# Last k tile of the first chunk tile by tile, evacuations ahead of low parts, a halved first cast, and more slots in a side list: one hybrid layer on one Trainium2 core

## The chip, the cores and the metric

The kernel runs on one core of one Trainium2 chip (trn2). The metric is the device time of one launch in microseconds (us); lower is better. All arithmetic is fp32. Products are made exact enough by splitting each fp32 operand into a high part (rounded to the format fp32r, one pass through TensorE) and a low part (the remainder), and by adding three products: high x high, high x low and low x high.

## The reference, cut to what matters

One layer over 1024 prompt tokens and 64 sample tokens (8 sequences of 8), model width 1024:

```
h    = rmsnorm(x, g_norm)                       # 1088 tokens x 1024
proj = h @ w_in                                 # 3200 columns = 25 tiles of 128
bg, cg, v, zA, a, g, zB, q, zX = split(proj)
out_A = bg * dwconv3(cg * v) * silu(zA)
out_B = silu(layernorm(dwconv31(a * sigmoid(g)))) * silu(zB)
out_X = softmax(q k^T / 8) v * silu(zX)         # 4 heads, 256 memory tokens
y     = rmsnorm(x + concat(out_A, out_B, out_X) @ w_out, g_final)
```

The prompt's keys and values come from `mem_prompt`; each of the eight sample sequences has its own cached keys and values. The states of both convolutions and the prompt's keys and values are outputs too.

## The kernel before, in words

**Tiles.** The projection is computed transposed: an accumulator in PSUM holds 128 output columns by a chunk of tokens, and eight k tiles of 128 input channels are summed in it. The first four column tiles ("head", `NHEAD`; three of kind `a`, one of kind `g`) go over four token chunks of 256, 256, 256 and 320 (`HEAD`); the other 21 over three of 384, 384 and 320 (`REST`). Per tile and chunk TensorE makes 24 matmuls: pass 0 is high weights x high tokens (rows `mm<-hh,wh`), pass 1 low weights x high tokens (`mm<-hh,wl`), pass 2 high weights x low tokens (`mm<-hl,wh`). `pass_k(n, c, acc, p, k)` is one of them. PSUM has eight banks: four for these accumulators (`MM`, rows named `mm`) and four for everything else (`SD`, rows named `sd`).

**Who does what.** TensorE (PE) also transposes the tokens (`x_tr`, rows `sd<-ident,x`). ScalarE (ACT) takes such a bank and writes the high part `hh` (`x_ev_hi`), VectorE (DVE) the low part `hl` (`x_ev_lo`). Weights are loaded in fp32 (`wr`); a CAST makes `wh` and VectorE the remainder `wl`. For the first four column tiles the weights come per k tile: `hw_hi(k)` casts 128x512, columns of all four tiles side by side, and `hw_lo(k)` subtracts. Only k tile 0 is cast by VectorE, the others by ScalarE (`S.copy`).

**The start.** `startup()` (L1007) is written out by hand, and each engine runs its part of it in the order of the code. Chunks 0 and 1 are multiplied without their norm factor; it is applied when an accumulator is emptied. For this `r_bc` makes diagonal matrices of the factors on VectorE, `r_tr` transposes them on TensorE, and a copy puts the row into `rrow`; `evac` of a head tile in chunks 0 and 1 is then one VectorE multiplication by `rrow` (rows `u<-mm,rrow` for the three tiles of kind `a`, `sig<-mm,rrow` for the `g` tile). `n0` and `n1` are the norms of chunks 0 and 1: `square(i)` is a ScalarE pass over one 128x1024 token tile (rows `junk<-x`), `chain` and `factor` are small VectorE operations. After chunk 0 has used its accumulators, chunk 1 gets the same four banks; its first matmul per tile thus waits for that tile's evacuation. Chunk 1 starts with pass 0 of all four tiles, k tile by k tile, with one pair of transposes (`x_tr(1, k + 4)`) behind each of the first four.

**The rest.** Outside `startup()` a list scheduler sets each engine's order from the code's order and readiness. Beside the main stream there is a queue of side steps: `side()` is called twice in each pass of eight matmuls (after k = 3 and k = 7) and runs the next entry; an entry `None` is an empty slot. The samples' attention is such a series, queued at column tile 14 (L1249): transposes of the cached keys (`sa_T`), `sa_scores`, `S0` empty slots, `sa_norm` (VectorE scales the softmax rows `Ps`), `S1` empty slots, `sa_pT` (TensorE transposes `Ps`, VectorE copies the result to `Pts`), `S2` empty slots, `sa_pv` (product with the cached values, ScalarE copies to `Os`), `S3` empty slots, `sa_out` (TensorE transposes `Os`). `st_out`, the output of the convolution states, is queued behind it. The 31 taps of the long convolution are VectorE operations on 128x1024 (rows `accB<-u,prm,accB`), a few per tile.

Of the kernel before, what the change touches and what calls it, by code (L numbers as in the profile page):

```python
# [23 lines left out]
SCALE = 0.125  # L24
NBIG = 45
A0, A1, A2, A3, A4, A5 = 2, 9, 5, 3, 3, 1
S0, S1, S2, S3 = 4, 3, 4, 2
L0, L1, L2 = 1, 3, 2
T1, T2, T3 = 2, 2, 3
TAPPRI = 100  # L30
# [11 lines left out]
def hybrid_trunk_kernel(  # L42
# [32 lines left out]
    def nm(s):  # L75
        uid[0] += 1
        return f"{s}_{uid[0]}"

    def B(s, dt=F32, cols=NT):
        return big.tile([128, cols], dt, tag="b", name=nm(s))  # L80

    def SD():
        return sdp.tile([128, 512], F32, tag="s", name=nm("sd"))

    def MM():
        return mmp.tile([128, 512], F32, tag="m", name=nm("mm"))
# [7 lines left out]
    def mm(out, lhsT, rhs, start, stop, cost):  # L94
        T.matmul(out, lhsT, rhs, start=start, stop=stop)  # L95
        pe_t[0] += cost
# [4 lines left out]
    def tr(out, in_, n):  # L101
        T.transpose(out, in_, ident[:n, :n])  # L102
        pe_t[0] += 107

    def dv(ns):
        dve_t[0] += ns
# [128 lines left out]
    def x_tr(c, k):  # L235
        off, n = HEAD[c]
        ps = SD()
        for i in groups[c]:
            o = xcols[i] - off
            tr(ps[:, o:o + 128], xt[i][:, k * 128:(k + 1) * 128], 128)  # L240
        return ps

    def x_ev(c, k, ps):
        x_ev_hi(c, k, ps)
        x_ev_lo(c, k, ps)

    def x_ev_hi(c, k, ps):
        off, n = HEAD[c]
        S.activation(hh[k][:, off:off + n], ps[:, :n], AF.Copy, scale=gT[:, k:k + 1])  # L249

    def x_ev_lo(c, k, ps):
        off, n = HEAD[c]
        V.scalar_tensor_tensor(
            hl[k][:, off:off + n], ps[:, :n], gT[:, k:k + 1],
            hh[k][:, off:off + n].bitcast(F32), ALU.mult, ALU.subtract,
        )
        dv(n / 0.96 + 130)
# [14 lines left out]
    hrw, hwh, hwl = [None] * 4, [None] * 4, [None] * 4  # L272

    def hsl(k):
        return slice((k % 2) * 512, (k % 2) * 512 + 512)
# [7 lines left out]
    def hw_hi(k, copy):  # L283
        if k % 2 == 0:
            hwh[k // 2] = B("wh", F32R, D)
            hwl[k // 2] = B("wl", F32R, D)
        copy(hwh[k // 2][:, hsl(k)], hrw[k // 2][:, hsl(k)])  # L287

    def hw_lo(k):
        V.tensor_sub(hwl[k // 2][:, hsl(k)], hrw[k // 2][:, hsl(k)], hwh[k // 2][:, hsl(k)].bitcast(F32))  # L290
# [2 lines left out]
    def w_block(n, k, lo):  # L293
        if n < NHEAD:
            o = (k % 2) * 512 + n * 128
            return (hwl if lo else hwh)[k // 2][:, o:o + 128]
        return (wlo if lo else whi)[n][:, k * 128:(k + 1) * 128]
# [95 lines left out]
    def chunks(n):  # L393
        return HEAD if n < NHEAD else REST
# [108 lines left out]
    def ev_z(c, ps, kk, src):  # L503
        off, n, p, s = pieces(c)
        if c[0] == 0:
            sz[0] = B("sz")
            mh[kk] = B("mh", F32R, SEQ)
            ml[kk] = B("ml", F32R, SEQ)
        m = src[:, off:off + n]
        S.activation(sz[0][:, off:off + n], ps[:, :n], AF.Silu)  # L510
        V.tensor_tensor(m, sz[0][:, off:off + n], m, ALU.mult)
        S.copy(mh[kk][:, off:off + p], m[:, :p])
        V.tensor_sub(ml[kk][:, off:off + p], m[:, :p], mh[kk][:, off:off + p].bitcast(F32))
        dv(2 * n / 0.96 + 140)
        if s:
            hi = ms[0][:, kk * 128:kk * 128 + 64]
            lo = ms[0][:, kk * 128 + 64:kk * 128 + 128]
            S.copy(hi, m[:, p:n])
            V.tensor_sub(lo, m[:, p:n], hi.bitcast(F32))
            dv(140)  # L520

    def evac(n, c, ps):
        kind, j, _ = order[n]
        c = chunks(n)[c]
        rawc[0] = n < NHEAD and c[0] < RAW
        if kind == "zA":
            ev_z(c, ps, j, tA[j])
        elif kind == "zB":
            ev_z(c, ps, 3 + j, accB[j])
        elif kind == "zX":  # L530
            ev_z(c, ps, 6 + j, aO[j])
        else:
            {"g": ev_g, "a": ev_a, "q": ev_q, "cg": ev_cg, "v": ev_v, "bg": ev_bg}[kind](c, ps, j)

    def pass_k(n, c, ps, p, k, last=2):
        off, N = chunks(n)[c]
        h = hl if p == 2 else hh
        mm(
            ps[:, :N], w_block(n, k, p == 1), h[k][:, off:off + N],
            p == 0 and k == 0, p == last and k == KT - 1, N / 2.4,  # L540
        )
# [465 lines left out]
    def startup():  # L1007
# [25 lines left out]
        n0, n1, n2, n3 = (Norm([xt[i] for i in g], [xrows[i] for i in g]) for g in groups)  # L1033
# [3 lines left out]
        def r_bc(norm, off):  # L1037
            norm.chain()
            norm.factor()
            for i in (0, 1):  # L1040
                o = off + i * 128
                V.tensor_scalar(rrow[0][:, o:o + 128], ident, 0.0, norm.f[:, i:i + 1], ALU.mult, ALU.add)
            dv(500)
# [20 lines left out]
        def p(k, j):  # L1064
            for n in range(NHEAD):
                pass_k(n, 0, acc[n], j, k, 1)
# [7 lines left out]
        def late(k):  # L1074
            banks.append(SD())
            for i in (0, 1):
                x0_tr(k, i)

        hw_hi(0, V.tensor_copy)
        hi(0)  # L1080
        hi(1)
# [3 lines left out]
        for i in (0, 1):  # L1085
            x0_tr(3, i)
        hw_hi(1, S.copy)
        lo(1)
        hw_lo(1)
# [4 lines left out]
        lo(2)  # L1094
        p(1, 0)
        hw_hi(2, S.copy)
        hw_lo(2)
        lo(3)
# [44 lines left out]
        t1 = [x_tr(1, 0), x_tr(1, 1)]  # L1143
# [4 lines left out]
        p(6, 1)  # L1148
        rps = r_tr(0)
        S.copy(rrow[0][:, RAW:RAW + 256], rps[:, :256])  # L1150
        n1.square(0)
        t1 += [x_tr(1, 2), x_tr(1, 3)]
        p(7, 0)
        x_ev(1, 2, t1[2])
        x_ev(1, 3, t1[3])
        n1.square(1)
        for n in range(NHEAD):
            for j in (2, 1):
                pass_k(n, 0, acc[n], j, KT - 1, 1)
            evac(n, 0, acc[n])  # L1160
        acc = [MM() for _ in range(NHEAD)]
        for k in range(KT):
            if k > 3:
                x_ev(1, k, t1[k])
            for n in range(NHEAD):
                pass_k(n, 1, acc[n], 0, k)
            if k + 4 < KT:
                t1.append(x_tr(1, k + 4))
            if k == 3:
                r_bc(n1, 256)  # L1170
        n2.square(0)
        n2.square(1)
        n2.chain()
# [23 lines left out]
    if True:  # L1197
        with tc.manual_schedule():
            startup()
# [16 lines left out]
        for n in range(NHEAD, NCT):  # L1216
            w_load(n + 2)
            kind, j, _ = order[n]
# [137 lines left out]
```

## Time and profile before

| what | value |
|---|---|
| median of 3 runs (lowest to highest) | 473.11 us (472.13 to 474.51) |
| the profiled execution | 472.01 us |
| its span, first to last instruction | 470.2 us |
| mean granted TensorE clock | 0.996 |
| busy: PE / weight loads (PEld) / DVE / ACT | 459.7 / 435.1 / 333.4 / 229.5 us |
| chain that ended last, by engine | PE 86%, DVE 11%, DMA 1%, issue 1%, ACT 1% |

The profiled execution lies 1.1 us under the median, and 1.8 us of it lie outside the span. PEld is the loading of the stationary operand, which overlaps the matmuls. Times in the rows are us from the span's start; a row of the timeline gives start, duration, engine, line of the code, operation, output<-inputs, shapes and count, and in brackets how long the engine sat idle before it and what ended that. All VectorE instructions are issued through one wrapper and stand at L59, nearly all matmuls at L95, transposes at L102.

### The profile page before, as it was taken

The numbers are of one execution on the slowest core, as the hardware profiler recorded it, in microseconds if no ns is written. First come the engines' busy times: TensorE is split into PE (matmuls) and PEld (weight loads), VectorE is DVE, ScalarE is ACT, GpSimd is POOL, SyncE is SP. The second block draws the span as 40 slices with busy tenths as digits, with TensorE's granted clock in tenths as the row PEclk, the third lists the DMA queues.
The fourth block names the chain that finished last, engine by engine and source line by source line (L and its number), as shares of the span: only waits on it lengthen the run. The fifth ranks groups of instructions, "written<-read, shape, count | busy, mean of one in ns | idle before, by whom it ended". The sixth has DMA issues, their size and how long they took to land.

```text
span 470.2 us, 7495 instructions
## 1 busy us (share of the span) xinstructions
PE 459.7 (98%) x2931; PEld 435.1 (93%) x2931; DVE 333.4 (71%) x593; ACT 229.5 (49%) x584; POOL 4.2 (1%) x20
## 2 busy tenths in 40 slices
PE   8999999999999999999999989999999999999994
PEld 8899999999999999999999879999999888888884
DVE  4769999999878999996899965237353537333333
ACT  5785659600223648565795364595542534111112
POOL 2000000000000000000000000000000000000000
PEclk9999999999999999999999999999999999999998
DMA  8931253100460300422021102113401634311111
GB/s 295 370 93 46 71 153 91 45 1 0 128 187 16 119 1 1 135 57 80 12 79 46 43 3 62 45 46 105 164 2 45 233 147 129 118 45 46 45 67 68
DMA packets 36447, 40.44 MB, mean 86 GB/s; under 512 B 1743, under 2 KB 30453, under 8 KB 36405
## 3 DMA queue, kind: packets, MB, share of 16 engines
q1 hardware_dynamic: 35965, 39.21, 25.7%
q10 hardware_dynamic: 448, 0.76, 0.5%
q8 instruction: 23, 0.38, 0.3%
q14 instruction: 11, 0.09, 0.1%
HBM read 34.81 MB, written 5.42 MB: 86 GB/s over the span
## 4 chain that ended last, share of the span: by engine, by line
PE 86%; DVE 11%; DMA 1%; issue 1%; ACT 1%; ACTq 0%; DVEq 0%
PE mm L95 76%; DVE accB L59 6%; PE sd L95 5%; PE sd L102 4%; DVE tA L59 1%; DVE wl L59 1%; DMA wr<-in_w_in_dram 1%; DVE red L59 1%; PE sd L874 1%; DVE mx L59 0%; DVE s L59 0%; ACT junk L187 0%; DVE hl L59 0%; ACT yg L997 0%; ACTq L1011 0%
## 5 line engine op out<-in xcount | busy, mean ns | idle before, releaser
L95 PE MATMUL mm<-hh,wh 128*128 128x384 f32 (+2 forms) x632 | 118.9, 324 | 1.1 <-DVE u L59 0.8
L95 PE MATMUL mm<-hl,wh 128*128 128x384 f32 (+2 forms) x632 | 118.6, 323 | 0.0
L59 DVE SCALAR_TENSOR_TENSOR accB<-u,prm,accB 128x1024 f32<-128x1024 f32 x90 | 115.4, 1282 | 1.5
L95 PE MATMUL mm<-hh,wl 128*128 128x384 f32 (+2 forms) x632 | 116.4, 321 | 0.0
L95 PEld LDWEIGHTS mm<-hh,wh 128*128 128x128 f32 x632 | 101.9, 188 | 2.8 <-DVE u L59 1.0
L95 PEld LDWEIGHTS mm<-hl,wh 128*128 128x128 f32 x632 | 101.7, 188 | 0.7 <-issue 0.6
L95 PEld LDWEIGHTS mm<-hh,wl 128*128 128x128 f32 x632 | 101.6, 188 | 0.4
L95 PE MATMUL mm<-woh,ml 128*128 128x512 f32 (+1 forms) x136 | 51.2, 377 | 0.0
L95 PE MATMUL mm<-wol,mh 128*128 128x512 f32 (+1 forms) x136 | 51.2, 377 | 0.0
L95 PE MATMUL mm<-woh,mh 128*128 128x512 f32 (+1 forms) x136 | 51.2, 377 | 0.0
L59 DVE TENSOR_TENSOR xres<-mm,xres 128x512 f32<-128x512 f32 (+2 forms) x19 | 12.4, 662 | 39.7 <-PE mm L95 39.5
L952 ACT ACTIVATE sd<-xres 128x512 f32<-128x512 f32 (+1 forms) x16 | 9.6, 600 | 57.9 <-DVE xres L59 57.9
L59 DVE TENSOR_TENSOR wl<-wr,wh 128x512 fp32r<-128x512 f32 x50 | 33.4, 688 | 4.2 <-ACT wh L287 2.2
L95 PEld LDWEIGHTS mm<-woh,mh 128*128 128x128 f32 x136 | 25.6, 188 | 4.7
L95 PEld LDWEIGHTS mm<-woh,ml 128*128 128x128 f32 x136 | 25.6, 188 | 4.7
L95 PEld LDWEIGHTS mm<-wol,mh 128*128 128x128 f32 x136 | 25.6, 188 | 4.6
L310 ACT CAST wh<-wr 128x512 fp32r<-128x512 f32 x42 | 24.4, 620 | 1.7 <-issue 1.3
L362 ACT ACTIVATE prod<-us,prm 128x64 f32<-128x64 f32 x93 | 24.9, 345 | 0.1
L510 ACT ACTIVATE sz<-mm 128x384 f32<-128x384 f32 (+1 forms) x24 | 11.4, 474 | 23.3 <-PE mm L95 23.1
L712 ACT ACTIVATE P<-sd,nb 128x256 f32<-128x256 f32 x32 | 14.7, 473 | 13.2 <-DVE nb L59 12.3
L433 ACT ACTIVATE sig<-mm 128x384 f32<-128x384 f32 (+1 forms) x6 | 2.8, 474 | 37.4 <-PE mm L95 37.3
L249 ACT ACTIVATE hh<-sd,gT 128x256 fp32r<-128x256 f32 (+1 forms) x32 | 14.3, 491 | 7.1 <-PE sd L102 6.8
(198 smaller groups left out, 527.9 us busy)
## 6 DMA issues: line engine op xcount, KB each, us to landing
wr<-in_w_in_dram SPq DMA_DIRECT2D x21, 512.0 KB
wor<-in_w_out_dram SPq DMA_DIRECT2D x8, 512.0 KB
xres<-in_x_prompt_dram SPq DMA_DIRECT2D x8, 512.0 KB
out_dram<-xres SPq DMA_DIRECT2D x7, 512.0 KB
x<-in_x_prompt_dram SPq DMA_DIRECT2D x6, 512.0 KB
cache<-in_cache_mem_k_dram SPq DMA_DIRECT2D x8, 256.0 KB
cache<-in_cache_mem_v_dram SPq DMA_DIRECT2D x8, 256.0 KB
wr<-in_w_in_dram SPq DMA_DIRECT2D x6, 256.0 KB
```

Source lines behind the costliest of these rows:

```text
L59: r = f(*a, **k)
L95: T.matmul(out, lhsT, rhs, start=start, stop=stop)
L102: T.transpose(out, in_, ident[:n, :n])
L249: S.activation(hh[k][:, off:off + n], ps[:, :n], AF.Copy, scale=gT[:, k:k + 1])
L310: S.copy(dst_hi[:, a:b], src[:, a:b])
L362: S.activation(p3[:, k, :], src, AF.Copy, scale=w[:, k0 + k:k0 + k + 1])
L433: S.activation(sig[j][:, off:off + n], ps[:, :n], AF.Sigmoid)
L510: S.activation(sz[0][:, off:off + n], ps[:, :n], AF.Silu)
L712: S.activation(P_[i][:, h * 256:h * 256 + 256], bank[h // 2][:, (h % 2) * 256:(h % 2) * 256 + 256], AF.Exp, bias=nb[:, h:h + 1], scale=SCA ...
L874: T.transpose(ps[:, j * 128:j * 128 + 128], accB[j][:, lncols[i]:lncols[i] + 128], ident)
L952: S.activation(junk[:rows], xr[:rows, cs], AF.Square, accum_out=ss[:rows, f:f + 1])
```

## The change

Three edits. (1) `hw_hi(0)`, the first weight cast, is made as two casts of 128x256. (2) In `startup()` the last k tile of chunk 0 (k = 7) is no longer pass 0 of all four tiles followed by passes 2 and 1 tile by tile, but all three passes tile by tile. The transposes of chunk 1's k tiles 2 and 3 stand ahead of it and behind its first tile. The low parts of those two (`x_ev_lo`) stand behind the four evacuations, the two squares of `n1` move back (the second to behind k = 4 of chunk 1), and `r_bc(n1, 256)` moves behind chunk 1's pass 0. (3) `S1` goes from 3 to 7 and `S2` from 4 to 6.

```diff
--- before.py
+++ after.py
@@ -24,7 +24,7 @@
 SCALE = 0.125
 NBIG = 45
 A0, A1, A2, A3, A4, A5 = 2, 9, 5, 3, 3, 1
-S0, S1, S2, S3 = 4, 3, 4, 2
+S0, S1, S2, S3 = 4, 7, 6, 2
 L0, L1, L2 = 1, 3, 2
 T1, T2, T3 = 2, 2, 3
 TAPPRI = 100
@@ -284,7 +284,11 @@
         if k % 2 == 0:
             hwh[k // 2] = B("wh", F32R, D)
             hwl[k // 2] = B("wl", F32R, D)
-        copy(hwh[k // 2][:, hsl(k)], hrw[k // 2][:, hsl(k)])
+        c0 = (k % 2) * 512
+        for a in (range(c0, c0 + 512, 256) if k == 0 else ()):
+            copy(hwh[0][:, a:a + 256], hrw[0][:, a:a + 256])
+        if k:
+            copy(hwh[k // 2][:, hsl(k)], hrw[k // 2][:, hsl(k)])
 
     def hw_lo(k):
         V.tensor_sub(hwl[k // 2][:, hsl(k)], hrw[k // 2][:, hsl(k)], hwh[k // 2][:, hsl(k)].bitcast(F32))
@@ -1148,16 +1152,18 @@
         p(6, 1)
         rps = r_tr(0)
         S.copy(rrow[0][:, RAW:RAW + 256], rps[:, :256])
-        n1.square(0)
-        t1 += [x_tr(1, 2), x_tr(1, 3)]
-        p(7, 0)
-        x_ev(1, 2, t1[2])
-        x_ev(1, 3, t1[3])
-        n1.square(1)
+        t1.append(x_tr(1, 2))
+        x_ev_hi(1, 2, t1[2])
         for n in range(NHEAD):
-            for j in (2, 1):
+            for j in (0, 2, 1):
                 pass_k(n, 0, acc[n], j, KT - 1, 1)
+            if n == 0:
+                t1.append(x_tr(1, 3))
+                x_ev_hi(1, 3, t1[3])
+                n1.square(0)
             evac(n, 0, acc[n])
+        x_ev_lo(1, 2, t1[2])
+        x_ev_lo(1, 3, t1[3])
         acc = [MM() for _ in range(NHEAD)]
         for k in range(KT):
             if k > 3:
@@ -1166,8 +1172,9 @@
                 pass_k(n, 1, acc[n], 0, k)
             if k + 4 < KT:
                 t1.append(x_tr(1, k + 4))
-            if k == 3:
-                r_bc(n1, 256)
+            if k == 4:
+                n1.square(1)
+        r_bc(n1, 256)
         n2.square(0)
         n2.square(1)
         n2.chain()
```

TensorE at the last k tile of chunk 0. The accumulators are mm_40 to mm_43; `hh_27`, `hl_28` are k tile 7's tokens, `sd_75`/`sd_76` before and `sd_74`/`sd_75` now the transposes of chunk 1's k tiles 2 and 3. Before:

```order
L102 MATMUL sd_76_374<-ident_72,x_6_109 128x128
L102 MATMUL sd_76_374<-ident_72,x_8_114 128x128
L95 MATMUL mm_40_168<-hh_27_138,wh_62_309 128x256
L95 MATMUL mm_41_169<-hh_27_138,wh_62_309 128x256
L95 MATMUL mm_42_170<-hh_27_138,wh_62_309 128x256
L95 MATMUL mm_43_171<-hh_27_138,wh_62_309 128x256
L95 MATMUL mm_40_168<-hl_28_139,wh_62_309 128x256
L95 MATMUL mm_40_168<-hh_27_138,wl_63_310 128x256
L95 MATMUL mm_41_169<-hl_28_139,wh_62_309 128x256
L95 MATMUL mm_41_169<-hh_27_138,wl_63_310 128x256
L95 MATMUL mm_42_170<-hl_28_139,wh_62_309 128x256
L95 MATMUL mm_42_170<-hh_27_138,wl_63_310 128x256
```

Now:

```order
L102 MATMUL sd_74_370<-ident_72,x_6_109 128x128
L102 MATMUL sd_74_370<-ident_72,x_8_114 128x128
L95 MATMUL mm_40_168<-hh_27_138,wh_62_310 128x256
L95 MATMUL mm_40_168<-hl_28_139,wh_62_310 128x256
L95 MATMUL mm_40_168<-hh_27_138,wl_63_311 128x256
L102 MATMUL sd_75_377<-ident_72,x_6_109 128x128
L102 MATMUL sd_75_377<-ident_72,x_8_114 128x128
L95 MATMUL mm_41_169<-hh_27_138,wh_62_310 128x256
L95 MATMUL mm_41_169<-hl_28_139,wh_62_310 128x256
L95 MATMUL mm_41_169<-hh_27_138,wl_63_311 128x256
L95 MATMUL mm_42_170<-hh_27_138,wh_62_310 128x256
L95 MATMUL mm_42_170<-hl_28_139,wh_62_310 128x256
```

The second pair of transposes moved behind the first tile's three matmuls, and each accumulator is complete three matmuls after the one before it.

VectorE at the same place; `u` and `sig` are the evacuations, `hl_18` and `hl_20` the low parts of chunk 1's k tiles 2 and 3. Before:

```order
L59 TENSOR_TENSOR wl_63_310<-wr_7_111,wh_62_309 128x512
L59 SCALAR_TENSOR_TENSOR hl_14_125<-sd_71_343,gT_74,hh_13_124 128x256
L59 SCALAR_TENSOR_TENSOR hl_16_127<-sd_72_346,gT_74,hh_15_126 128x256
L59 SCALAR_TENSOR_TENSOR hl_18_129<-sd_75_371,gT_74,hh_17_128 128x256
L59 SCALAR_TENSOR_TENSOR hl_20_131<-sd_76_374,gT_74,hh_19_130 128x256
L59 TENSOR_TENSOR u_78_389<-mm_40_168,rrow_35_155 128x256
L59 TENSOR_TENSOR u_79_394<-mm_41_169,rrow_35_155 128x256
L59 TENSOR_TENSOR u_80_399<-mm_42_170,rrow_35_155 128x256
L59 TENSOR_TENSOR sig_81_404<-mm_43_171,rrow_35_155 128x256
```

Now:

```order
L59 TENSOR_TENSOR wl_63_311<-wr_7_111,wh_62_310 128x512
L59 SCALAR_TENSOR_TENSOR hl_14_125<-sd_71_344,gT_74,hh_13_124 128x256
L59 SCALAR_TENSOR_TENSOR hl_16_127<-sd_72_347,gT_74,hh_15_126 128x256
L59 TENSOR_TENSOR u_77_383<-mm_40_168,rrow_35_155 128x256
L59 TENSOR_TENSOR u_78_389<-mm_41_169,rrow_35_155 128x256
L59 TENSOR_TENSOR u_79_395<-mm_42_170,rrow_35_155 128x256
L59 TENSOR_TENSOR sig_80_401<-mm_43_171,rrow_35_155 128x256
L59 SCALAR_TENSOR_TENSOR hl_18_129<-sd_74_370,gT_74,hh_17_128 128x256
L59 SCALAR_TENSOR_TENSOR hl_20_131<-sd_75_377,gT_74,hh_19_130 128x256
```

Two low parts stood ahead of the four evacuations and now stand behind them.

TensorE at the samples' softmax, column tiles 17 (its last chunk, 128x320) and 18 (128x384). Before, the two pairs of transposes of `Ps` stand within pass 2 of tile 17's last chunk:

```order
L95 MATMUL mm_3120<-hl_129,wh_2860 128x320
L95 MATMUL mm_3120<-hl_131,wh_2860 128x320
L102 MATMUL sd_3144<-ident,Ps_3079 128x128 x2
L95 MATMUL mm_3120<-hl_133,wh_2860 128x320
L95 MATMUL mm_3120<-hl_135,wh_2860 128x320
L95 MATMUL mm_3120<-hl_137,wh_2860 128x320
L95 MATMUL mm_3120<-hl_139,wh_2860 128x320
L102 MATMUL sd_3153<-ident,Ps_3086 128x128 x2
```

Now they stand within pass 1 of tile 18's first chunk:

```order
L95 MATMUL mm_3157<-hh_128,wl_3052 128x384
L95 MATMUL mm_3157<-hh_130,wl_3052 128x384
L102 MATMUL sd_3170<-ident,Ps_3080 128x128 x2
L95 MATMUL mm_3157<-hh_132,wl_3052 128x384
L95 MATMUL mm_3157<-hh_134,wl_3052 128x384
L95 MATMUL mm_3157<-hh_136,wl_3052 128x384
L95 MATMUL mm_3157<-hh_138,wl_3052 128x384
L102 MATMUL sd_3179<-ident,Ps_3087 128x128 x2
```

Between the two places lie 16 matmuls: the last four of 128x320 and twelve of 128x384. `sa_pv`, `sa_out` and `st_out` move by six slots (24 matmuls). Behind this place ScalarE's order has the copies `Os` behind the two casts of tile 19's weights, where they stood ahead of them. From column tile 19 on the order of every engine is as before.

## The prediction

> **What bounds the kernel now.** I read the page first (busy time, chain), then PE's waits, then busy time by stretch, and last the timeline at each wait.
>
> ```profile
> PE 459.7 (98%) x2931; PEld 435.1 (93%) x2931; DVE 333.4 (71%) x593; ACT 229.5 (49%) x584; POOL 4.2 (1%) x20
> PE 86%; DVE 11%; DMA 1%; issue 1%; ACT 1%; ACTq 0%; DVEq 0%
> ```
>
> PE is busy for 459.7 of 470.2 us. None of the edits removes a matmul, so all that can be won is PE's idle time, 10.5 us, or time that passes for busy.
>
> ```profile
> PE sd L102 <- DVE Ps L59: 1.3, 1, 1.3
> PE mm L95 <- DVE u L59: 0.8, 1, 0.8
> PE mm L95 <- DVE wh L59: 0.3, 1, 0.3
> PE sd L102 <- ACT rrow L1150: 0.2, 1, 0.2
> ```
>
> Columns: who waited for whom, us in total, times, longest. They are the places of the three edits: the first cast (`wh`), the copy of `rrow` and the evacuations (`u`) at the end of chunk 0, and the samples' softmax (`Ps`).
>
> ```profile
> core 0: us, PE busy (x) PEld busy (x) DVE busy (x) ACT busy (x) POOL busy (x), PEclk, DMA share, GB/s
> 18.30:36.80 18.50, 17.41 (x140) 16.32 (x139) 13.87 (x40) 15.07 (x31) 0.00 (x0) 1.00 0.48 150
> 36.80:58.40 21.60, 21.60 (x173) 21.37 (x174) 20.95 (x44) 11.80 (x28) 0.00 (x0) 1.00 0.20 58
> 58.40:225.00 166.60, 166.60 (x1075) 163.77 (x1076) 153.45 (x217) 81.52 (x230) 0.20 (x2) 1.00 0.24 72
> 225.00:260.00 35.00, 35.00 (x271) 34.07 (x270) 34.50 (x43) 25.17 (x75) 0.10 (x1) 1.00 0.16 46
> 260.00:275.00 15.00, 14.23 (x110) 12.68 (x108) 14.79 (x21) 8.47 (x14) 0.00 (x0) 1.00 0.13 36
> 287.00:464.00 177.00, 176.86 (x958) 160.66 (x956) 77.97 (x182) 69.13 (x170) 0.00 (x0) 1.00 0.25 85
> ```
>
> From 36.8 to 260 us PE has no idle time, and from 287 to 464 us only 0.14. What is won at the start reaches the end if DVE, as full as PE from 225 on (34.50 of 35.00 us), follows.
>
> **Edit 1, the first cast in halves.**
>
> ```profile
> 5.78 0.84 ACT L249 ACTIVATE hh<-sd,gT 128x256 fp32r<-128x256 f32 x2 [2.05 <-PE sd L102]
> 5.94 0.43 DVE L59 CAST wh<-wr 128x512 fp32r<-128x512 f32 x1 [0.37 <-DMA wr<-in_w_in_dram]
> 6.28 0.48 DVE L59 SCALAR_TENSOR_TENSOR hl<-sd,gT,hh 128x256 fp32r<-128x256 f32 x1
> 6.51 0.72 PE L95 MATMUL mm<-hh,wh 128*128 128x256 f32 x4 [0.34 <-DVE wh L59]
> 7.29 0.62 ACT L287 CAST wh<-wr 128x512 fp32r<-128x512 f32 x1 [0.67 <-DMA wr<-in_w_in_dram]
> 8.12 0.55 PEld L95 LDWEIGHTS mm<-hh,wh 128*128 128x128 f32 x4
> ```
>
> The cast ends at 6.37 and the first matmul starts 0.14 later. No row shows a cast of 256; it lies between half of 0.43 and 0.43 whole, about 0.29. The first half then ends at 6.23, so PE starts by up to 0.14 earlier (`hh` is ready at about 6.2). But the next weights are cast on ACT, which waited for their DMA and ends at 7.91; with the same 0.1 of signalling their LDWEIGHTS cannot come before 8.02, where it now comes at 8.12. So 0.10 is left of it. What waits behind the second half on DVE is `hl`: it starts before its predecessor has ended (6.28 against 6.37), so it slips by some 0.07, and PE needs it only later. Ends: 0.15 if the second half delays what follows by its whole length, turned into a loss (+0.15), and 0.34, the whole idle time. I take -0.10, the bound that the next cast's row sets.
>
> [...]
>
> **Edit 2, the last k tile of chunk 0.**
>
> ```profile
> 18.12 0.69 DVE L59 TENSOR_TENSOR wl<-wr,wh 128x512 fp32r<-128x512 f32 x1
> 18.43 0.38 PE L102 MATMUL sd<-ident,x 128*128 128x128 f32 x2
> 18.62 0.37 ACT L1150 COPY rrow<-sd 128x256 f32<-128x256 f32 x1 [1.07 <-PE sd L102]
> 18.72 0.87 DVE L59 SCALAR_TENSOR_TENSOR hl<-sd,gT,hh 128x256 fp32r<-128x256 f32 x2
> 18.89 1.06 ACT L187 ACTIVATE junk<-x 128x1024 f32<-128x1024 f32 x1
> 19.05 0.44 PE L102 MATMUL sd<-ident,x 128*128 128x128 f32 x2 [0.24 <-ACT rrow L1150]
> 20.45 0.88 DVE L59 SCALAR_TENSOR_TENSOR hl<-sd,gT,hh 128x256 fp32r<-128x256 f32 x2 [0.85 <-ACT hh L249]
> 21.24 1.08 DVE L59 TENSOR_TENSOR u<-mm,rrow 128x256 f32<-128x256 f32 x3
> 21.71 1.38 PE L95 MATMUL mm<-hh,wh 128*128 128x256 f32 x4 [0.80 <-DVE u L59]
> 22.23 0.42 DVE L59 TENSOR_TENSOR sig<-mm,rrow 128x256 f32<-128x256 f32 x1
> 22.93 0.38 PE L102 MATMUL sd<-ident,x 128*128 128x128 f32 x2
> 23.06 0.71 PE L95 MATMUL mm<-hh,wh 128*128 128x256 f32 x4
> ```
>
> The chain: a square on ACT (18.89) holds up the high parts, those hold up two low parts on DVE (idle 0.85, then 20.45), those the evacuations (21.24 on), and PE waits 0.80 for the first. Its next four matmuls take 1.38 against 0.71 for four at 23.06: they too come one evacuation apart, 0.33, which the idle column doesn't show.
>
> Now the same rows in the new order, in the old times. Transposes at 18.43, three matmuls at 18.65, 18.77 and 18.89 (0.12 apart: 256 columns against the 384 that take 1.48 for eight at 276.54 below), the third just behind `wl` (18.12 + 0.69 = 18.81). The second pair of transposes waits for the copy of `rrow` as before and stays at 19.05. The nine matmuls behind it run from 19.24 and complete the second, third and fourth accumulator at about 19.85, 20.20 and 20.55 (a result some 0.3 after its matmul's start: 0.71 for four at 23.06, less three steps). DVE is free at 19.50, since only the first two low parts (18.72) stand ahead. Evacuations: 19.50, then 19.90, 20.25 and 20.60 as the accumulators come, the last done at 21.02. PE, through with chunk 0 at 20.4, needs the fourth bank last: its matmul starts at 21.08 and the next transposes at 21.30 instead of 22.93. That is **-1.6**. Ends: with no wait at all PE would be there at about 20.95 (-2.0); if the evacuations ran one after another only behind PE's last matmul (20.61 to 22.0, transposes at 22.3), -0.6. I take the middle one because each of its terms is a row.
>
> What stands behind what: the two low parts moved back are done at about 21.8, and PE needs their banks for transposes only two steps on (22.7). The second square (1.06, and 0.2 for its accumulator) now stands on ACT ahead of the high part of k tile 5; that part is done at about 23.5 and PE comes to it at 24.5, so it is hidden, by 1.0. `r_bc` for chunk 1 is needed after 32 matmuls of pass 1 and has 3.8 us of cover. A pair of transposes and a matmul swap places later on; that costs nothing as both are ready.
>
> **Edit 3, the slots.**
>
> ```profile
> 224.29 1.29 DVE L59 TENSOR_REDUCE mx<-sd 128x2 f32<-128x512 f32 x2 [3.02 <-PE sd L95]
> 275.07 0.62 DVE L59 TENSOR_SCALAR Ps<-Ps,rc 128x256 f32<-128x256 f32 x2
> 275.57 0.41 PE L102 MATMUL sd<-ident,Ps 128*128 128x128 f32 x2 [1.34 <-DVE Ps L59]
> 276.54 1.64 PE L95 MATMUL mm<-hh,wh 128*128 128x384 f32 x8
> 278.02 1.55 PE L95 MATMUL mm<-hh,wl 128*128 128x384 f32 x8
> ```
>
> PE stands from 274.23 (275.57 less the 1.34) to 275.57 for the softmax that DVE finishes. Sixteen matmuls now go first: eight of 384 go from 276.54 to 278.02, 1.48, of which the first few tenths are the transposes' tail, so I take 0.16 each; twelve are 1.9, and four of 320, narrower, at 0.13 are 0.5: 2.4 us, more than the wait. **-1.34**, and `sa_pT` would have a margin of 1.1. DVE's 3.02 us of idle time at 224.29, for PE's scores, shows that its full stretch begins with PE: it starts earlier by as much as PE does. The copies `Pts` and `Os` come later too, but six slots of four matmuls lie between `sa_pT` and `sa_pv`. No queue of SP or POOL changes its order; buffers are handed out differently (below).
>
> **Sum.** 0.10 + 1.6 + 1.34 = 3.0 us. The profiled execution would go from 472.01 to 469.0, its span to about 467.2. The median before is 473.11, 1.1 above that execution; I put the same 3.0 on it: **470.1 us**, 0.64% faster. A measurement of this kernel tells about 0.5% (2.4 us) from no change. The likeliest case's own range is 469.4 (edit 1 at -0.34, edit 2 at -2.0) to 471.3 (at +0.15 and -0.6).
>
> [...] By idle time alone edit 2 would be worth 0.24 + 0.80 = 1.04, and the sum 2.5.
>
> **Rivals.**
> - *The start's gain is lost on the way, the softmax's stays*: 473.1 - 1.34 = 471.8. From 36.8 to 58.4 DVE is busy for 20.95 of 21.60 us; if it does not come earlier with PE, new waits for low parts appear there. Against: its work there comes from PE's transposes, which move. 0.20.
> - *The softmax's wait moves with its step*: if DVE falls behind by more than the 1.1 of margin, for it does 14.79 of 15.00 us there, PE waits again; 473.1 - 1.7 = 471.4. 0.10.
> - *Neither arrives*, 473.1: 0.06.
> - *Slower.* ACT now makes the casts of tile 19's weights ahead of the copies `Os`, and these hold PE's transposes of `Os`.
>
> ```profile
> 267.30 0.37 SPq L304 DMA_DIRECT2D wr<-in_w_in_dram  x1
> 281.29 0.37 SPq L304 DMA_DIRECT2D wr<-in_w_in_dram  x1
> 281.41 0.37 ACT L821 COPY Os<-sd 128x256 f32<-128x256 f32 x1 [3.17 <-PE sd L95]
> 284.65 1.14 ACT L310 CAST wh<-wr 128x512 fp32r<-128x512 f32 x2
> ```
>
>   Tile 19's load was issued at 267.30, tile 20's at 281.29, right as `sa_pv` let go of its cache. Were tile 19's load to get such a buffer, it would be issued behind the later `sa_pv`, at about 282.5; with some 3.5 for 512 KB, 1.14 for the casts and 0.8 for two copies PE could go on at 288, where without that it is there at 284.2. A loss of 3.8 against 3.0 gained: 473.9. It decides from an issue later than 281.7. Against: 14 us between the two issues. 0.04.
>
> **Chances.** The likeliest has 0.60; the five make 1.0. The range of 469.0 to 472.4 holds the likeliest with 0.4 of scatter below it and the first two rivals, and leaves out the last two and the tails. Faster by over 0.5% means under 470.7: most of the likeliest, 0.56. Slower by over 0.5% (475.5) takes more than the last rival gives: 0.03. Within: 0.41.
>
> **What the profile after would show.** Right: PE's wait for `Ps` gone; the wait for `u` gone or under 0.2, and the four matmuls behind it under 1.1; the pair of transposes now at 22.93 at about 21.2; the first matmul at about 6.4. Wrong: new waits of PE for `hl` or `hh` between 21 and 60 us, for `Ps` or `Os` near 270 to 285, or ends that have not moved although the waits are gone.

## The result and the profile after

| kernel | median us (lowest to highest) | ratio to before, 95% interval |
|---|---|---|
| before, same chip | 472.82 (472.13 to 474.51) | 1 |
| changed | 469.77 (469.50 to 470.41) | 0.9937 [0.9919, 0.9955] |

The changed kernel is 3.05 us faster, 0.63%, against 3.0 forecast. The profiled execution of it took 469.5 us with a span of 467.7 (before 470.2). Of 63 executions of the kernel before in all series, 14 lay 1.4 us or more above their series' median (as the 474.51 here), and 1 of 33 of the kernels with edit 2 whole and S1 at 5 or 7; no trace was kept of one, so the cause is open.

The page of the changed kernel, busy time and the shares of the chain that ended last:

```profile
PE 459.0 (98%) x2931; PEld 435.2 (93%) x2931; DVE 332.9 (71%) x594; ACT 228.6 (49%) x584; POOL 4.1 (1%) x20
PE 97%; DMA 1%; ACT 0%; DVE 0%; ACTq 0%; issue 0%
```

PE's work is the same, and VectorE's 11% of the chain are gone. PE's waits (who for whom, us in total, times, longest):

```profile
PE mm L1035 <- POOL ss L182: 1.4, 1, 1.4
PE mm L95 <- DVE wh L59: 0.7, 1, 0.7
PE mm L95 <- ACT wh L291: 0.3, 1, 0.3
```

The first line is the same in every kernel, before included. Those for `Ps`, `u` and `rrow` are gone. The wait for `wh`, which edit 1 aims at, is longer than before (0.7 against 0.3), and a wait for k tile 1's weights is new. Busy time by stretch (columns as in the prediction):

```profile
18.30:34.00 15.70, 15.70 (x131) 15.38 (x130) 12.47 (x38) 13.59 (x29) 0.00 (x0) 1.00 0.59 183
222.20:257.20 35.00, 35.00 (x272) 34.07 (x271) 33.53 (x43) 25.70 (x76) 0.10 (x1) 1.00 0.16 46
257.20:272.20 15.00, 15.00 (x117) 13.71 (x116) 14.75 (x19) 7.37 (x12) 0.00 (x0) 1.00 0.13 36
272.20:284.20 12.00, 12.00 (x94) 10.76 (x93) 7.42 (x18) 6.46 (x16) 0.00 (x0) 1.00 0.05 14
```

PE has no idle time left in any of them.

The timeline of the changed kernel at the last k tile of chunk 0 (edit 2), to be read beside the rows from 18.43 to 23.06 in the prediction:

```profile
18.95 0.38 PE L102 MATMUL sd<-ident,x 128*128 128x128 f32 x2
19.25 0.87 DVE L59 SCALAR_TENSOR_TENSOR hl<-sd,gT,hh 128x256 fp32r<-128x256 f32 x2
20.04 1.16 DVE L59 TENSOR_TENSOR u<-mm,rrow 128x256 f32<-128x256 f32 x3
20.43 1.05 ACT L187 ACTIVATE junk<-x 128x1024 f32<-128x1024 f32 x1
20.93 1.07 PE L95 MATMUL mm<-hh,wh 128*128 128x256 f32 x4
21.13 0.42 DVE L59 TENSOR_TENSOR sig<-mm,rrow 128x256 f32<-128x256 f32 x1
21.47 0.86 DVE L59 SCALAR_TENSOR_TENSOR hl<-sd,gT,hh 128x256 fp32r<-128x256 f32 x2
21.84 0.38 PE L102 MATMUL sd<-ident,x 128*128 128x128 f32 x2
...
223.20 1.29 DVE L59 TENSOR_REDUCE mx<-sd 128x2 f32<-128x512 f32 x2 [3.02 <-PE sd L95]
```

This execution enters the place 0.52 late (transposes at 18.95 where before has 18.43) and leaves it 1.09 early (21.84 against 22.93). The square (`junk`) starts at 20.43, behind the high parts that it held up before, and the two low parts at 21.47 stand behind the four evacuations. The last row, 200 us on, is the `mx` of the prompt's last scores: 223.20 against 224.29, still 1.09 early. At the samples' softmax `Ps` is as early (273.98 against 275.07), so the gain travelled there whole.

The same view at the softmax and behind it (edit 3):

```profile
265.33 0.37 SPq L308 DMA_DIRECT2D wr<-in_w_in_dram  x1
...
273.98 0.61 DVE L59 TENSOR_SCALAR Ps<-Ps,rc 128x256 f32<-128x256 f32 x2
274.98 0.86 PE L95 MATMUL mm<-hh,wl 128*128 128x384 f32 x4
275.67 0.38 PE L102 MATMUL sd<-ident,Ps 128*128 128x128 f32 x2
...
281.99 0.37 SPq L308 DMA_DIRECT2D wr<-in_w_in_dram  x1
283.84 0.37 ACT L825 COPY Os<-sd 128x256 f32<-128x256 f32 x1 [0.49 <-PE sd L95]
285.62 0.38 PE L102 MATMUL sd<-ident,Os 128*128 128x128 f32 x2
```

`Ps` is done at 274.59 and PE takes it at 275.67: the margin of 1.1 that was forecast. Tile 19's weights were issued at 265.33, far ahead of `sa_pv`; tile 20's, at 281.99, waited for tile 19's `wl` (done at 281.96) and no longer for `sa_pv` as in before. PE took `Os` at 285.62 without waiting.

**One way of reading used below.** In every profile the start of the same instruction is taken at five points, which cuts the span into four stretches. The points are the first head matmul (before: 6.51), the transposes `sd<-ident,x` ahead of chunk 0's last k tile (18.43), the first pair behind chunk 1's first four matmuls (22.93), the `mx` row (224.29), and the end of the span (470.2). All lengths in us:

| kernel | first matmul | to 18.43's pair | edit 2's stretch | to `mx` | `mx` to the end (edit 3) |
|---|---|---|---|---|---|
| before | 6.51 | 11.92 | 4.50 | 201.36 | 245.9 |
| changed | 6.48 | 12.47 | 2.89 | 201.36 | 244.5 |
| start only | 6.91 | 12.23 | 2.88 | 201.38 | 246.0 |
| slots only | 6.95 | 11.91 | 4.49 | 201.36 | 244.5 |
| cast only | 7.11 | 11.91 | 4.50 | 201.36 | 245.9 |
| without the cast | 7.67 | 11.95 | 2.87 | 201.39 | 244.5 |
| low parts ahead | 7.40 | 11.91 | 3.69 | 201.38 | 244.5 |
| before with S1 = 4 | 7.64 | 11.91 | 4.50 | 201.39 | 245.4 |
| changed with S1 = 5, S2 = 4 | 6.76 | 11.94 | 2.87 | 201.38 | 244.7 |
| weights first | 6.84 | 11.94 | 2.87 | 201.36 | 244.5 |
| weights first, again | 6.55 | 12.04 | 2.88 | 201.37 | 244.5 |
| changed, again | 6.55 | 12.00 | 2.88 | 201.38 | 244.6 |

In the third and fourth column of numbers kernels with the same code at that place agree to 0.03 us, and in the last, whose ends are rounded, to 0.1. The first column moves by 1.2 us between executions, for reasons of its own (below). The second is 11.91 at the least, and longest where PE waits for k tile 1's weights (12.47, 12.23). What PE is late by at 18.43's pair passes through to the end, as the columns behind it show.

### The profile page after: what moved, and what is told of

The parts are those of the page before. It is cut to its first block, busy times and chain, and to the rows that moved or that the text cites. A ratio compares the mean times of both kernels' runs of the same rounds, so it can differ in the third digit from the quotient of the medians.

```text
span 467.7 us, 7495 instructions
## 1 busy us (share of the span) xinstructions
PE 459.0 (98%) x2931; PEld 435.2 (93%) x2931; DVE 332.9 (71%) x594; ACT 228.6 (49%) x584; POOL 4.1 (1%) x20
## 4 chain that ended last, share of the span: by engine, by line
PE 97%; DMA 1%; ACT 0%; DVE 0%; ACTq 0%; issue 0%
PE mm L95 84%; PE sd L95 6%; PE sd L102 6%; DMA wr<-in_w_in_dram 1%; PE sd L878 1%; ACT yg L1001 0%; ACT wh L291 0%; ACTq L1015 0%; ACT sd L986 0%; DVE xres L59 0%; DVE t L59 0%; ACTq L281 0%; PE sd L852 0%; PE sd L847 0%; ACT y L993 0%
## 5 line engine op out<-in xcount | busy, mean ns | idle before, releaser
L59 DVE TENSOR_TENSOR accB<-sz,accB 128x384 f32<-128x384 f32 (+1 forms) x9 | 4.8, 535 | 17.3 <-ACT sz L514 17.3
```

Of the source, the lines that this page charges most:

```text
L59: r = f(*a, **k)
```

## The experiments

Theory: edits 2 and 3 each give what PE waited for, and the parts add up. Rivals: the gains overlap, or one of them is lost on the way; edit 1 decides something.

**Start only**: edit 2 alone, that is the changed kernel with this taken back.

```diff
-S0, S1, S2, S3 = 4, 7, 6, 2
+S0, S1, S2, S3 = 4, 3, 4, 2
-        c0 = (k % 2) * 512
-        for a in (range(c0, c0 + 512, 256) if k == 0 else ()):
-            copy(hwh[0][:, a:a + 256], hrw[0][:, a:a + 256])
-        if k:
-            copy(hwh[k // 2][:, hsl(k)], hrw[k // 2][:, hsl(k)])
+        copy(hwh[k // 2][:, hsl(k)], hrw[k // 2][:, hsl(k)])
```

> The kernel before with edit 2 alone (last k tile of chunk 0 tile by tile, evacuations ahead of the low parts). Theory (each edit takes away the wait at its own place, and what is won there is kept): 1.6 us, ratio about 0.9966; the transposes behind the evacuations come 1.6 earlier against the place just ahead of them, every row from 25 to 270 us is earlier by the same, and PE still waits 1.3 for Ps. Rival (VectorE's full stretch from 225 us on does not follow): PE waits about 2.9 for Ps and the time is as before.

Measured: 471.11 us (470.44 to 473.04) against 472.79 for before, ratio 0.9963 [0.9948, 0.9979]. PE's waits:

```profile
PE mm L1031 <- POOL ss L182: 1.4, 1, 1.4
PE sd L102 <- DVE Ps L59: 1.3, 1, 1.3
PE mm L95 <- ACT hh L249: 0.4, 1, 0.4
```

The 0.4 for `hh` stand ahead of the first matmul, which starts 0.57 behind the cast as in the other kernels with the whole cast, so the cast was what came last. The wait for `Ps` keeps its 1.3. The softmax comes earlier together with PE and does not eat the start's gain.

**Slots only**: edit 3 alone.

```diff
-S0, S1, S2, S3 = 4, 3, 4, 2
+S0, S1, S2, S3 = 4, 7, 6, 2
```

> The kernel before with edit 3 alone (S1 = 7, S2 = 6). Theory: the wait for Ps goes, 1.34 to 1.5 us, ratio about 0.997; nothing ahead of 270 us moves. Rival (the slots only pay once the start is faster, or a wait for Os takes the place): a wait of PE of over 0.5 at Ps, Pts or Os, and less than 0.8 us.

Measured: 471.34 us, ratio 0.9973 [0.9958, 0.9987]. Its waits:

```profile
PE mm L1031 <- POOL ss L182: 1.4, 1, 1.4
PE mm L95 <- DVE u L59: 0.8, 1, 0.8
PE sd L102 <- ACT rrow L1150: 0.2, 1, 0.2
```

`Ps` is gone, `u` and `rrow` stay. By medians the two parts give 1.68 and 1.45, together 3.13.

**Cast only**: edit 1 alone.

```diff
-        copy(hwh[k // 2][:, hsl(k)], hrw[k // 2][:, hsl(k)])
+        c0 = (k % 2) * 512
+        for a in (range(c0, c0 + 512, 256) if k == 0 else ()):
+            copy(hwh[0][:, a:a + 256], hrw[0][:, a:a + 256])
+        if k:
+            copy(hwh[k // 2][:, hsl(k)], hrw[k // 2][:, hsl(k)])
```

> The kernel before with edit 1 alone (first cast in halves). Theory: at most 0.1 us, not to be told from none; PE's first matmul starts about 0.14 earlier after the landing of its weights than now, and the next weights' load sets when k tile 1 starts. Rival (fixed cost of a second instruction on VectorE): the low parts behind it come 0.15 later and PE waits for wl, slower by up to 0.15. In the profile of after the two halves took 0.49 together, against 0.43 for the whole.

Measured: 473.01 us against 472.79 for before, ratio 1.0003 [0.9987, 1.0019].

```profile
6.67 0.49 DVE L59 CAST wh<-wr 128x256 fp32r<-128x256 f32 x2 [1.10 <-DMA wr<-in_w_in_dram]
7.08 0.48 DVE L59 SCALAR_TENSOR_TENSOR hl<-sd,gT,hh 128x256 fp32r<-128x256 f32 x1
7.11 0.71 PE L95 MATMUL mm<-hh,wh 128*128 128x256 f32 x4 [0.71 <-DVE wh L59]
```

From the start of the cast to the first matmul there are 0.44 us, where the whole cast has 0.57 (5.94 to 6.51 in the prediction's rows). So the edit did save 0.13, but the weights landed 0.73 later in this execution, which hides it.

**Without the cast**: edits 2 and 3, no edit 1 (the cast's lines taken back as in the first experiment, the slots left at 7 and 6).

> The changed kernel without edit 1. Theory: the same time as the changed kernel within 0.1 us plus the scatter of the first loads, so about 3.0 us under before, ratio 0.9937. If the halved cast were worth more than 0.4 us, this run would lie above 470.1.

Measured: 469.64 us, ratio 0.9928 [0.9913, 0.9944], the same as the full change. Edits 2 and 3 carry all that the medians can tell; what edit 1 adds lies under the scatter.

**Low parts ahead**: the changed kernel with the two low parts back ahead of the evacuations, the matmuls tile by tile as they are.

```diff
-        x_ev_hi(1, 2, t1[2])
+        x_ev(1, 2, t1[2])
...
-                x_ev_hi(1, 3, t1[3])
+                x_ev(1, 3, t1[3])
...
-        x_ev_lo(1, 2, t1[2])
-        x_ev_lo(1, 3, t1[3])
```

> The changed kernel with the two low parts of chunk 1's k tiles 2 and 3 ahead of the four evacuations again; the last k tile of chunk 0 stays tile by tile. Theory (the order on VectorE makes half of edit 2, the order on PE and ACT the other half): the first evacuation starts about 0.9 us later than in the changed kernel, the transposes behind the evacuations about 0.8 later, time about 0.8 above the changed kernel, 470.5. Rival (tile by tile alone does it): within 0.2 of the changed kernel. Other rival (only the order on VectorE matters): 1.4 or more above it.

Measured: 470.41 us (469.87 to 472.25), against 472.60 for before, ratio 0.9959 [0.9945, 0.9973].

```profile
19.60 1.79 DVE L59 SCALAR_TENSOR_TENSOR hl<-sd,gT,hh 128x256 fp32r<-128x256 f32 x4
21.32 1.07 DVE L59 TENSOR_TENSOR u<-mm,rrow 128x256 f32<-128x256 f32 x3
21.78 1.38 PE L95 MATMUL mm<-hh,wh 128*128 128x256 f32 x4 [0.34 <-DVE u L59]
23.00 0.38 PE L102 MATMUL sd<-ident,x 128*128 128x128 f32 x2
```

Four low parts run without a gap now (before, VectorE stood idle 0.85 between them), the evacuations follow, and PE's four matmuls come one evacuation apart again (1.38). The stretch is 3.69, between 4.50 and 2.89: matmul order and the later square together are worth 0.81, the low parts behind the evacuations another 0.80. No run separates the first two. The rows point at the square: without VectorE's gap of 0.85 the evacuations start 2.01 behind the pair of transposes instead of 2.81, and in the old matmul order too each accumulator would have been done by its turn (the last at 20.91 in before, 2.48 behind the pair, its turn here at about 3.0). By that reading the tile-by-tile order earns its share only together with the low parts' move, which lets VectorE begin 1.09 behind the pair.

**S1 = 4 alone**, in the kernel before: is the wait for `Ps` paid off by matmuls, at their own rate?

```diff
-S0, S1, S2, S3 = 4, 3, 4, 2
+S0, S1, S2, S3 = 4, 4, 4, 2
```

> The kernel before with S1 = 4 in place of 3, all else as before. Theory (PE's wait for Ps shrinks by the matmuls that go first): one slot is four matmuls of 128x320, about 0.55 us, so the wait goes from 1.34 to about 0.8 and the gain is about 0.55. Rival (the wait follows its step): still 1.3, no gain.

Measured: 472.15 us, ratio 0.9993 [0.9984, 1.0002]; by medians 0.45 less, within its interval no difference. The trace is sharper than the clock here:

```profile
276.71 0.41 PE L102 MATMUL sd<-ident,Ps 128*128 128x128 f32 x2 [0.75 <-DVE Ps L59]
```

The wait went from 1.34 to 0.75, the last stretch from 245.9 to 245.4. One slot is four matmuls, and the wait shrank by 0.59, what four matmuls of 128x320 take.

**S1 = 5, S2 = 4**, in the changed kernel: are the other two slots of S1, and those of S2, worth anything?

```diff
-S0, S1, S2, S3 = 4, 7, 6, 2
+S0, S1, S2, S3 = 4, 5, 4, 2
```

> The changed kernel with S1 = 5 and S2 = 4 in place of 7 and 6. Theory: two slots are 0.55 + 0.65 = 1.2 us, a wait for Ps of 0.1 to 0.2 is left and the time is that of the changed kernel within 0.2; the other two slots and S2 are worth nothing. Rival (S2 or the last two slots carry part of the gain): 0.4 or more above the changed kernel, with a wait at Ps or Pts.

Measured: 469.78 us (469.00 to 470.01), ratio 0.9938 [0.9926, 0.9950], the same as the full change (0.9937). In its trace:

```profile
273.31 0.88 PE L95 MATMUL mm<-hh,wh 128*128 128x384 f32 x4
274.22 0.41 PE L102 MATMUL sd<-ident,Ps 128*128 128x128 f32 x2
```

The transposes start 0.91 behind four matmuls of 384 that elsewhere have the next instruction 0.69 behind them (274.98 to 275.67 above): some 0.2 are still lost, with no wait listed, as the last matmul's tail covers it (the four end, as modelled, at 274.19). Two slots do nearly all the work.

**Weights first**: in the changed kernel, k tile 0's weights are issued ahead of the norm's gains on ScalarE's queue.

```diff
         x_half(0, 0, nc.sync)
+        hw_load(0, nc.scalar)
         nc.scalar.dma_start(graw, g_norm[0].rearrange("(k p) -> k p", p=128))
         x_half(1, 0, nc.sync)
-        hw_load(0, nc.scalar)
```

> The changed kernel with the first weight load issued ahead of the load of the norm's gains on ACT's queue, about 0.6 us earlier. Theory (after the change the start is bound by when the weights of k tile 0 and 1 land): PE's first matmul 0.3 to 0.6 earlier, the time 0.3 to 0.6 below the changed kernel. Rival (the 16 DMA engines are full, so the order only moves bytes among the first loads): the first matmul earlier, but k tile 1's or the tokens' landing later, no change of time.

Measured: 469.31 us (468.92 to 469.81), ratio 0.9931 [0.9918, 0.9944].

```profile
5.48 0.48 DVE L59 CAST wh<-wr 128x256 fp32r<-128x256 f32 x2
5.80 0.79 PEld L102 LDWEIGHTS sd<-ident,x 128*128 128x128 f32 x5 [0.33 <-DMA x<-in_x_prompt_dram]
6.32 0.84 ACT L249 ACTIVATE hh<-sd,gT 128x256 fp32r<-128x256 f32 x2 [2.65 <-PE sd L102]
6.84 0.73 PE L95 MATMUL mm<-hh,wh 128*128 128x256 f32 x4
```

The cast starts at 5.48, but the first matmul waits for the high part, whose tokens landed late in this execution, and comes at 6.84, no earlier than the 6.48 of the changed kernel's trace. Tokens that late occur with the old order too (a wait of 1.07 for `x` in the run without the cast), so this one trace does not put it on the order of the loads. As 469.31 was the lowest median so far, it was timed once more beside the changed kernel on one chip.

**Weights first, again.** 

> The changed kernel with the load of k tile 0's weights issued ahead of the load of the norm gains on ScalarE's queue, timed once more, on the same chip as the changed kernel itself. In nine profiled executions with the old order of the loads the first matmul started between 6.48 and 7.67 us, 7.05 in the mean; in the one with the new order at 6.84, held by the high part and no longer by the weights. Theory (the order of the loads takes out the late landings of the weights): the first matmul at about 6.8 again, and a time 0.2 to 0.4 below the changed kernel's of the same call. Rival (the x tile's landing only takes over, the mean stays): the same time as the changed kernel within 0.1.

**Changed, again.** 

> The changed kernel as it is, as the partner of the run before it. Both theories expect 469.8 +- 0.3. If the weights of k tile 0 land last, the first matmul stands 0.44 behind the start of the first cast, as in all three such executions with halves (0.57 with the whole cast, in four); if the high part is last, 0.52 behind its start.

Measured: 469.31 us (469.12 to 471.14), ratio 0.9927 [0.9904, 0.9950], and 469.45 us (469.25 to 469.68), ratio 0.9921 [0.9903, 0.9939], before at 472.67. They differ by 0.14, under the 0.2 of the theory and over the 0.1 of its rival, in intervals that overlap, so the two are not told apart; both first matmuls stand at 6.55. In the changed kernel:

```profile
5.91 0.49 DVE L59 CAST wh<-wr 128x256 fp32r<-128x256 f32 x2 [0.34 <-DMA wr<-in_w_in_dram]
6.02 0.90 ACT L249 ACTIVATE hh<-sd,gT 128x256 fp32r<-128x256 f32 x2 [2.29 <-PE sd L102]
6.55 0.74 PE L95 MATMUL mm<-hh,wh 128*128 128x256 f32 x4
```

Here the high part was last (0.53 from its start to the matmul), so the halves earned nothing. No version beats the changed kernel by more than can be told.

## Why the prediction was right, and where its terms were off

**Edit 2, forecast -1.6, measured -1.61 in the stretch** (4.50 to 2.89; 2.87 to 2.89 in seven executions). The steps hold one by one once the 0.52 by which this execution came late is taken off: evacuations from 19.52 (20.04 less 0.52; forecast 19.50), the last from 20.61 (forecast 20.60), the transposes at 21.32 (forecast 21.30), the four matmuls 1.07 long (forecast under 1.1). The estimate from idle time alone was 1.04, and is refuted. The starts of PE's instructions give the whole of it. One row of before and one of now, beside those shown:

```profile
20.63 0.28 PE L95 MATMUL mm<-hh,wl 128*128 128x256 f32 x1
```

```profile
19.77 0.37 PE L95 MATMUL mm<-hh,wh 128*128 128x256 f32 x1
```

Before, chunk 0's last matmul starts at 20.63, so at 0.12 each PE could have gone on at 20.75 and stood until 21.71: 0.96, of which the idle column lists 0.80. The two pairs of transposes with the wait for `rrow` took 0.81 (18.43 to 19.24) and take 0.30 now (18.95 to 19.09, 19.61 to 19.77): 0.51 less, where the column lists 0.24. The four matmuls behind the evacuations, counted as busy, go from 1.38 to 1.07: 0.31. The twelve of k tile 7 take 0.17 more, 1.68 against 1.51. That is 0.96 + 0.51 + 0.31 - 0.17 = 1.61. The trace counts those 0.31 of waiting as busy.

One term behind it was mis-sized without effect: the second square was to be hidden by 1.0, but the high part of k tile 5 was done at 24.13 and PE came to it at 24.62, so it was hidden by 0.5.

**Edit 3, forecast -1.34, measured -1.5 at the softmax and -1.4 to the end.** The term was slightly too small because it took the idle column for the loss. The kernel before, last matmuls ahead of the wait:

```profile
272.31 1.34 PE L95 MATMUL mm<-hh,wl 128*128 128x320 f32 x8
273.48 0.75 PE L95 MATMUL mm<-hl,wh 128*128 128x320 f32 x4
```

Eight start 1.17 apart from the next eight, so four take 0.59, and the transposes could have started at 274.07. The idle time is counted from 274.23, when the last result is modelled as done. The loss is 275.57 - 274.07 = 1.50. At 292 us, with the transposes of `accB`, PE had gained 1.52 on the place ahead of the softmax in the changed kernel and 1.51 in the slots-only one; from 385 us on it is 1.42 to 1.43. Which work in between takes the 0.1 was not looked for. The margin of 1.1 came out as forecast by two sizes that were both too small: the sixteen matmuls took 2.69 (272.98 to 275.67) and not 2.4, and the loss was 1.50 and not 1.34.

**Edit 1, forecast -0.10 with ends of +0.15 and -0.34.** The mechanism stands: cast to matmul went from 0.57 (0.57 to 0.58 in four executions with the whole cast) to 0.44 (three with halves), 0.13 where "up to 0.14" was forecast, and a half takes 0.29, as estimated. It counts only where the first weights land last. In the profiled execution they did, but k tile 1's weights landed later still:

```profile
6.04 0.49 DVE L59 CAST wh<-wr 128x256 fp32r<-128x256 f32 x2 [0.83 <-DMA wr<-in_w_in_dram]
6.45 0.48 DVE L59 SCALAR_TENSOR_TENSOR hl<-sd,gT,hh 128x256 fp32r<-128x256 f32 x1
6.48 0.71 PE L95 MATMUL mm<-hh,wh 128*128 128x256 f32 x4 [0.67 <-DVE wh L59]
7.99 0.62 ACT L291 CAST wh<-wr 128x512 fp32r<-128x512 f32 x1 [1.74 <-DMA wr<-in_w_in_dram]
8.66 0.74 PE L95 MATMUL mm<-hh,wh 128*128 128x256 f32 x4 [0.31 <-ACT wh L291]
```

That is the bound the prediction set from the next cast's row, and here it took more than the gain: at 8.66 PE lost 0.46 (four matmuls from 7.72 on let it go on at 8.20), and by chunk 0's end it was 0.52 late. From the first matmul to the pair of transposes the halves cost nothing (11.91 in cast only as in slots only). So edit 1 is worth between 0 and 0.13 in these traces, and no median shows it. The 0.29 for a half stands in no row of before; it was the author's estimate between half of 0.43 and 0.43 whole. The changed kernel's trace shows 0.29 for each half, but the two take 0.49 together, so they overlap by 0.09, and `hl` starts 0.41 behind the cast's start against 0.34 before, a slip of 0.07. The end of +0.15 is shown by no run: the two halves are 0.06 longer than the whole cast.

**The rivals.** *Gain lost on the way*: refuted, the 201.36 us from the start to `mx` are the same in every kernel within 0.03. *The softmax's wait moves with its step*: refuted, margin 1.1. *Slower by `Os`*: the load came at 265.33, far from 281.7. *Neither arrives*: refuted by the parts.

**The sum.** Forecast 3.0, measured 3.05 by medians, in part by luck: edit 1's 0.10 is shown by no run, and edit 3 gave 0.1 more than its term. The profiled execution was to take 469.0 and took 469.5; the difference is the 0.52 by which PE came late at the start. The forecast's 0.33 above the measured 469.77 is nearly all in the base: before had 473.11 in the runs shown and 472.82 beside the changed kernel.

## What to carry to other kernels

Complete accumulators one after another, empty each at once, and put nothing ahead of that on the emptying engine, or on the engine that feeds it, that is needed later (here 1.61 us, of which the low parts' move made 0.80). A wait of the bounding engine for another engine's chain is paid off by moving the consumer behind ready work, at the rate of that work (here 0.59 for four matmuls); count the loss from the starts of instructions, not from the idle column (here two slots left 0.2, four left nothing). Where a change is under 1%, cut the trace into stretches between instructions of the same name: the parts here repeat to 0.1 us there, while medians of the same kernel move by 0.3.

## What the runs showed of the hardware that was not expected

The start's scatter. With the same order of loads, the first cast, which waits for its DMA in each of them, began between 5.89 and 7.07 us, and the first matmul between 6.48 and 7.67 (ten executions of kernels whose start up to there differs at most in the halved cast). Up to chunk 0's last k tile a wait for k tile 1's weights can take part of it (12.47 from the first matmul to there in the changed kernel, where 11.91 is the least); from there on it reaches the end whole (to `mx` 201.36 to 201.39 behind edit 2's stretch, whatever the start). A scatter of 1.2 us hides edit 1's 0.13 and comes near each of the other two edits. Which of the loads lands last changes too: the weights (in cast only the first cast waited 1.10 for them), the tokens (in the kernel without the cast a wait of 1.1 for `x`), or k tile 1's weights (in the changed kernel ScalarE waited 1.74 for them). Why they land so was not tried.

PE's idle column starts when the last matmul's modelled result is written: at the softmax in before 0.16 us behind the time at which the next could have started (274.23 against 274.07). The wait of 0.2 with S1 = 5 doesn't show in it at all.
